# Address offsets modulo 512 bytes for the float32r operands of a Winograd-type matmul, and other dummy products

## The chip, the cores and the metric

The kernel runs on one core of a Trainium2 chip. The metric is the device time of one execution in microseconds; a kernel's time is the median of several executions. A core has five engines that run side by side: TensorE (PE; its weight loads are shown as PEld), VectorE (DVE), ScalarE (ACT), GpSimd (POOL) and SyncE (SP, which here issues transfers). Operands lie in SBUF, 128 partitions wide; an address below is the byte within a partition. TensorE's results go to PSUM.

## The reference

```python
qkv = np.matmul(x, w_qkv)          # x [16, 512, 768], w_qkv [768, 2304], float32
q, k, v = the three column blocks of 768
return np.stack([q, k, v], axis=0)  # [3, 16, 512, 768], float32
```

So it is one product of 8192 x 768 by 768 x 2304, whose columns go to three blocks of the output.

## The kernel before

The 8192 rows of x are worked off in 32 tiles p of 256 rows. The columns of w are cut into two quads q of 1024 columns (two blocks c of 512 each) and a remainder of 256. A product of 256 rows by 768 by 1024 is seen as a 2 x 2 x 2 block product and computed with seven instead of eight half products (Strassen's scheme in Winograd's form). The seven need sums of blocks of x, `s` (five slices k of three parts j, each 128 x 128, float32r), and sums of blocks of w, `t_0` for the first quad and `t_1` for the second (four sums of 3 x 512 columns each, float32r). Two of the seven products use plain bfloat16 blocks (`xb` and `b1`); the other five use float32r: `s` against `t_0`, `t_1` or `b22`. In each, the slice of `s` or `xb` is the stationary operand (the weights that TensorE loads, 128 x 128) and 512 columns of the other are streamed. One half product is three such instructions, over j (lines 211 to 215). The remainder is a plain bfloat16 product (`rem`, line 262).

The first three tiles (`NS = 3`) are computed plainly in bfloat16 by `block` (line 385) while w comes in, since the sums of w aren't ready by then. Before that, dummy products of zeros (`busy`, line 365) keep TensorE going while the first rows arrive: `busy(11)`, then the transposes of the first rows (`turn_rows(0)`, line 167), `busy(4)`, then the casts and the transposes of the next rows (`turn_rows(1)`), then the products of line 385.

From tile 3 on, `two` runs both quads of a tile in an order written out by hand: the first bfloat16 product of each quad, the remainder, the second bfloat16 products, and then ten float32r half products, thirty instructions in a row. `early` issues the next tile's preparation: VectorE transposes x (line 130), POOL makes the bfloat16 copy (line 175) and the five operations of the sums (lines 183 to 187). `last` does the last tile in another order, so that its output can leave early.

The order on each engine is the program's own (the schedule is manual); transfers of w and x and most stores are issued by SP, later loads of x partly by ACT. Tiles are given out by pools in order; the width of 176 of the tile `eye` (line 75) brings all tiles behind it to multiples of 512 bytes:

```python
eye = w_pool.tile([P, 176], bf16, name="eye")[:, :P]
```

In the kernel before, every slice of `s`, `t_0`, `t_1` and `b22` starts at a multiple of 512 bytes: a slice of `s` is 128 float32r, thus 512 bytes, and a slice of the sums of w 2048 bytes.

Of the kernel before, what the change touches and what calls it, by code (L numbers as in the profile page):

```python
# [10 lines left out]
def kernel(  # L11
# [20 lines left out]
    nc = tc.nc  # L32
    P = 128
# [5 lines left out]
    KT = K // P  # L39
    KH = KT // 2  # L40
    KC = K // 4
    NP = M // (2 * P)
    CB = 512
    REM = N3 - 4 * CB
    Q_OFF = (0, 2 * CB + REM)
    R_OFF = 2 * CB
    fp32 = mybir.dt.float32
    f32r = mybir.dt.float32r
# [11 lines left out]
    tq_pool = ctx.enter_context(tc.tile_pool(name="tq", bufs=2))  # L60
    bt_pool = ctx.enter_context(tc.tile_pool(name="bt", bufs=1))
# [7 lines left out]
    s_pool = ctx.enter_context(tc.tile_pool(name="s", bufs=2))  # L69
# [5 lines left out]
    eye = w_pool.tile([P, 176], bf16, name="eye")[:, :P]  # L75
    w_rem = [w_pool.tile([P, KH, REM], bf16, name="w_rem0"), None]

    b1 = [w_pool.tile([P, KT, CB], bf16, name=f"b1_{q}") for q in range(2)]
    b22 = [w_pool.tile([P, KH, CB], f32r, name=f"b22_{q}") for q in range(2)]
    t_0 = w_pool.tile([P, 4, KH, CB], f32r, name="t_0")  # L80
    w_rem[1] = rem_pool.tile([P, KH, REM], bf16, name="w_rem1")
    ts = [[t_0[:, n] for n in range(4)], None]
# [4 lines left out]
    def load_w(dst, j0, nj, off, cols):  # L87
        rows = w_qkv.rearrange("(p j) n -> p j n", j=KT)
        nc.sync.dma_start(dst, rows[:, j0:j0 + nj, off:off + cols])
# [2 lines left out]

    def load_blocks(q, c, nj=KH):
        if q == 0:
            t = tq_pool.tile([P, KT, CB], fp32, name="st0", tag="tq")
            for j in range(0, KT, nj):
                load_w(t[:, j:j + nj], j, nj, Q_OFF[q] + c * CB, CB)
            stage[q, 0, c], stage[q, 1, c] = t[:, :KH, :], t[:, KH:, :]
        else:
            for h in range(2):  # L100
                t = st_pool.tile([P, KH, CB], fp32, name="st1", tag="st")
                load_w(t[:], h * KH, KH, Q_OFF[q] + c * CB, CB)
                stage[q, h, c] = t[:]
# [15 lines left out]
    def load_x(p, other):  # L119
        xin[p] = xin_pool.tile([P, 2 * P // G, KC], fp32, name="xin")  # L120
        t = xin[p]
        rows = x_flat[p * 2 * P:(p + 1) * 2 * P, :].rearrange("(g b) k -> b g k", b=G)
        for n in range(2):
            for h in range(2):
                i = 2 * h + n
                (nc.sync, other)[h].dma_start(t[i * G:(i + 1) * G], rows[:, :, i * KC:(i + 1) * KC])
# [26 lines left out]
    def cast_rows(p, two=True):  # L153
        src = xin.pop(p)
        xc[p] = s_pool.tile([P, 2, K], bf16, name="xc", tag="s")
        for r in range(2):
            halves = (slice(0, K // 2), slice(K // 2, K))
            copy_halves([xc[p][:, r, n] for n in halves], [src[:, r, n] for n in halves], two)

    def turn_rows(p, two=True):  # L160
        c = xc.pop(p)
        xb[p] = xb_pool.tile([P, KT, 2 * P], bf16, name="xb", tag="xb")
        for r in range(2):
            cols = c[:, r, :].rearrange("m (p j) -> m j p", j=KT)
            ps = ps_pool.tile([P, KT, P], bf16, name="ps")
            for j in range(KT):
                nc.tensor.transpose(ps[:, j, :], cols[:, j, :], eye)  # L167
            ks = (slice(0, KH), slice(KH, KT))
            copy_halves(
                [xb[p][:, n, r * P:(r + 1) * P] for n in ks], [ps[:, n, :] for n in ks], two  # L170
            )
# [5 lines left out]
    def sums_x(p):  # L177
        t = xf.pop(p)
        a11, a12 = t[:, :KH, :P], t[:, KH:, :P]
        a21, a22 = t[:, :KH, P:], t[:, KH:, P:]  # L180
        s = s_pool.tile([P, 5, KH, P], f32r, name="s")
        g = nc.gpsimd
        g.tensor_tensor(s[:, 1], a21, a22, op=add)  # L183
        g.tensor_tensor(s[:, 2], s[:, 1], a11, op=sub)  # L184
        g.tensor_tensor(s[:, 3], a11, a21, op=sub)  # L185
        g.tensor_copy(out=s[:, 0], in_=a22)
        g.tensor_tensor(s[:, 4], a12, s[:, 2], op=sub)  # L187
        sr[p] = s
# [5 lines left out]
    def quad(p, q):  # L194
        u = Quad()
        u.p, u.q = p, q
        u.o = o_pool.tile([P, 2, 2 * CB], fp32, name="o", tag="o")
        u.x = u.y = u.z = None
        return u
# [17 lines left out]
    def bank():  # L217
        return ps_pool.tile([P, CB], fp32, name="ps")
# [29 lines left out]
    def rows_of(s, p, lo, hi):  # L248
        return out_flat[s, p * 2 * P:(p + 1) * 2 * P, lo:hi].rearrange("(r m) n -> m r n", m=P)
# [10 lines left out]
    def rem_row(p, r, ps):  # L260
        for j in range(KT):
            nc.tensor.matmul(  # L262
                ps, xb[p][:, j, r * P:(r + 1) * P], w_rem[j // KH][:, j % KH, :],
                start=(j == 0), stop=(j == KT - 1), skip_group_check=True,
            )

    def rem(p):
        ps = ps_pool.tile([P, 2, REM], fp32, name="ps")
        for r in range(2):
            rem_row(p, r, ps[:, r, :])  # L270
        o = or_pool.tile([P, 2, REM], fp32, name="orem")
        nc.scalar.activation(o[:], ps[:], ident)  # L272
        nc.sync.dma_start(rows_of(1, p, R_OFF - H, R_OFF - H + REM), o[:])

# [67 lines left out]


    NS = 3
    zero = xb_pool.tile([P, CB], bf16, name="zero", tag="xb")
    nc.vector.memset(zero[:], 0.0)  # L346
    load_rows(0)
    nc.scalar.activation(tiny[:], zero[:, :1], ident)
    make_identity(nc, eye)
    load_rows(1)  # L350
    load_blocks(0, 0, 1)
    st_rem = o_pool.tile([P, KT, REM], fp32, name="str", tag="o")
    load_w(st_rem[:], 0, KT, R_OFF, REM)
    load_rows(2)
    load_blocks(0, 1)
    load_blocks(1, 0)
    load_blocks(1, 1)
    load_x(3, nc.sync)
    quads = [[quad(p, q) for p in range(NS)] for q in range(2)]

    def busy(n):

        ps = bank()
        for _ in range(n):
            nc.tensor.matmul(ps[:], zero[:, :P], zero[:], start=True, stop=True)  # L365

    def cast(q, h, c, w, eng):

        dst = w[:, h * KH:(h + 1) * KH, :]
        if eng is nc.scalar:  # L370
            eng.activation(dst, stage[q, h, c], ident)
        else:
            eng.tensor_copy(out=dst, in_=stage[q, h, c])
# [40 lines left out]

    nothing = lambda p: None
    busy(11)
    cast_rows(0)
    turn_rows(0)
    busy(4)
    cast_rows(1)  # L420
    cast_k(0)
    cast_k(1)
# [21 lines left out]
    block(1, 0, b1[1], halves(range(6)), cast_next(1, 1, bt1))  # L444
    block(1, 1, bt1, halves(range(6)), nothing)
    rem(2)
    t_1 = [tq_pool.tile([P, 2, KH, CB], f32r, name=f"t_1{n}", tag="tq") for n in range(2)]
    ts[1] = [t_1[n // 2][:, n % 2] for n in range(4)]
    sum_w(1, 1)
    sum_w(1, 2)  # L450
    transpose(3)
    round_x(3)
    sums_x(3)
    sum_w(1, 3)
    sum_w(1, 4)
    dve.tensor_copy(out=b22[1][:], in_=stage[1, 1, 1])

    for p in range(NS, NP):
        def early():
            if p + 1 < NP:  # L460
                transpose(p + 1)
                round_x(p + 1)
                sums_x(p + 1)
            if p + 2 < NP:
                load_x(p + 2, nc.scalar)

        if p < NP - 1:
            two(quad(p, 0), quad(p, 1), early)
        else:
            last(quad(p, 0), quad(p, 1))  # L470
# [30 lines left out]
```

## Time and profile before

| what | value |
|---|---|
| time, median of 3 runs (lowest to highest) | 363.17 us (362.58 to 363.25) |
| profiled execution: span from first to last instruction | 361.3 us |
| mean granted clock of TensorE | 1.000 |
| busy: TensorE / weight loads | 353.4 / 251.0 us |
| busy: VectorE / ScalarE / POOL | 224.4 / 182.9 / 173.9 us |
| float32r products (lines 211 to 215) | 696 + 174 |
| period of one tile in `two` | 10.74 us |

The profile is of one execution, and the page gives its span; its own time isn't listed beside the three runs, whose median is 1.87 us above that span. Busy time of TensorE is not a measure of work, because matmuls are pipelined and a matmul's length overlaps the next one's. The distance between the starts of two matmuls, or of the two weight loads that go with them, is what one costs. In the groups of instructions, a row names the line, the engine, the operation, the tiles written and read, shapes and count, then busy time in us, the mean length in ns, and the idle time in front.

### The profile page before, as it was taken

How to read it: one execution, taken by the hardware profiler on the slowest of the kernel's cores; microseconds unless marked ns; L12 is line 12 of the kernel's file. 1: busy time of each engine (PE TensorE's matmuls, PEld its weight loads, DVE VectorE, ACT ScalarE, POOL GpSimd, SP SyncE). 2: the span in 40 equal slices, each digit the busy share in tenths (PEclk: the TensorE clock that was granted, in tenths of full speed). 3: DMA queues.
4: the chain of work that ended last, by engine and by line, in shares of the span. 5: the costliest groups of instructions: out<-in, count | busy, mean ns of one | idle time of the engine just before them, and what ended most of it. 6: DMA issues, size and time to landing. Idle time of an engine off the chain costs nothing.

```text
span 361.3 us, 5221 instructions
## 1 busy us (share of the span) xinstructions
PE 353.4 (98%) x1765; PEld 251.0 (69%) x1797; DVE 224.4 (62%) x239; ACT 182.9 (51%) x304; POOL 173.9 (48%) x180
## 2 busy tenths in 40 slices
PE   8999999999999999999999999999999999999995
PEld 3644577777777777777777777777777777777763
DVE  3499826765566765566675565676556676556642
ACT  4547555455454545454545445455545454545452
POOL 0001861746664445664445665444665444666410
PEclk9999999999999999999999999999999999999999
DMA  7999869988898999899899999998989899999666
GB/s 298 405 388 373 286 221 359 331 289 295 278 328 301 294 273 294 276 324 315 280 280 290 281 308 309 291 289 278 292 288 321 295 300 271 297 272 339 264 261 232
DMA packets 80617, 108.08 MB, mean 299 GB/s; under 512 B 4816, under 2 KB 60368, under 8 KB 80592
## 3 DMA queue, kind: packets, MB, share of 16 engines
q1 hardware_dynamic: 65184, 96.35, 80.8%
q10 hardware_dynamic: 15408, 11.41, 9.6%
q8 instruction: 14, 0.23, 0.3%
q14 instruction: 11, 0.09, 0.1%
HBM read 32.24 MB, written 75.50 MB: 298 GB/s over the span
## 4 chain that ended last, share of the span: by engine, by line
PE 96%; ACT 1%; issue 1%; ACTq 0%; DVE 0%
PE ps L212 75%; PE ps L262 11%; PE ps L385 9%; PE ps L365 1%; PE ps L167 1%; ACT o L243 0%; ACTq L303 0%; ACT xb L147 0%; ACT orem L317 0%; DVE xb L145 0%; ACT xc L147 0%; ACTq L319 0%; DVE zero L346 0%; ACTq L317 0%
## 5 line engine op out<-in xcount | busy, mean ns | idle before, releaser
L212 PE MATMUL ps<-t,s 128*128 128x512 f32 x696 | 173.8, 398 | 0.0
L212 PEld LDWEIGHTS ps<-t,s 128*128 128x128 f32 x696 | 130.7, 188 | 29.7
L175 POOL CAST xb<-xf 128x1536 bf16<-128x1536 f32 x29 | 43.8, 1510 | 168.3 <-DVE xf L130 156.0
L240 DVE TENSOR_TENSOR o<-o,ps 128x512 f32<-128x512 f32 x58 | 39.9, 688 | 91.2 <-ACT o L239 91.2
L130 DVE STREAM_TRANSPOSE xf<-xin 128x1536 f32<-128x1536 f32 x29 | 85.5, 2950 | 3.7 <-DMA out_dram<-orem 2.1
L212 PE MATMUL ps<-b,xb 128*128 128x512 bf16 x320 | 82.4, 380 | 1.5
L239 ACT ACTIVATE o<-ps 128x512 f32<-128x512 f32 x58 | 34.8, 600 | 44.2 <-PE ps L212 44.2
L212 PEld LDWEIGHTS <-xb 128*128 128x128 bf16 x348 | 31.7, 98 | 35.6 <-issue 7.3
L233 ACT ACTIVATE o<-ps 128x512 f32<-128x512 f32 x58 | 34.9, 601 | 42.1 <-PE ps L212 39.4
L246 DVE TENSOR_TENSOR o<-o,ps 128x512 f32<-128x512 f32 x58 | 39.9, 688 | 21.3 <-PE ps L212 20.2
L212 PE MATMUL ps<-b,s 128*128 128x512 f32 x174 | 48.7, 389 | 0.0
L262 PE MATMUL ps<-w_rem,xb 128*128 128x256 bf16 x384 | 47.2, 273 | 0.0
L243 ACT ACTIVATE o<-ps 128x512 f32<-128x512 f32 x58 | 34.7, 599 | 24.1 <-PE ps L212 21.3
L226 ACT ACTIVATE o<-ps 128x512 f32<-128x512 f32 x58 | 34.7, 598 | 23.8 <-DVE o L246 20.6
L262 PEld LDWEIGHTS <-xb 128*128 128x128 bf16 x384 | 37.4, 98 | 11.2 <-issue 0.5
L230 DVE TENSOR_TENSOR o<-o,ps 128x512 f32<-128x512 f32 x58 | 36.5, 673 | 5.4 <-PE ps L212 4.1
L212 PEld LDWEIGHTS ps<-b,s 128*128 128x128 f32 x174 | 32.7, 188 | 6.8
L184 POOL TENSOR_TENSOR s<-s,xf 128x384 fp32r<-128x384 f32 x29 | 30.0, 1035 | 2.3
L183 POOL TENSOR_TENSOR s<-xf 128x384 fp32r<-128x384 f32 x29 | 30.9, 1064 | 0.0
L185 POOL TENSOR_TENSOR s<-xf 128x384 fp32r<-128x384 f32 x29 | 29.5, 1017 | 0.0
L187 POOL TENSOR_TENSOR s<-xf,s 128x384 fp32r<-128x384 f32 x29 | 29.5, 1016 | 0.0
L272 ACT ACTIVATE orem<-ps 128x512 f32<-128x512 f32 x31 | 18.5, 598 | 20.7 <-PE ps L262 19.5
(36 smaller groups left out, 129.4 us busy)
## 6 DMA issues: line engine op xcount, KB each, us to landing
out_dram<-o SPq DMA_DIRECT2D x62, 768.0 KB, 4.8
out_dram<-o SPq DMA_DIRECT2D x65, 256.0 KB, 4.1
xin<-in_x_dram SPq DMA_DIRECT2D x62, 192.0 KB, 6.9
xin<-in_x_dram ACTq DMA_DIRECT2D x54, 192.0 KB, 4.4
out_dram<-orem SPq DMA_DIRECT2D x31, 256.0 KB, 5.7
st<-in_w_qkv_dram SPq DMA_DIRECT2D x6, 768.0 KB, 13.1
xin<-in_x_dram SPq DMA_DIRECT2D x3, 768.0 KB, 5.7
st<-in_w_qkv_dram SPq DMA_DIRECT2D x6, 256.0 KB, 6.1
```

The lines of the kernel that those rows point to most:

```text
L130: nc.vector.transpose(t[:].rearrange("p j (g b) -> p g j b", b=G), xin.pop(p)[:].rearrange("p g (a j) -> p g j a", a=G),)
L175: nc.gpsimd.tensor_copy(out=xb[p][:], in_=xf[p][:])
L212: nc.tensor.matmul(ps[:], lhs[j], rhs[j], start=(start and j == 0), stop=(j == KH - 1), skip_group_check=True,)
L226: nc.scalar.activation(c11, u.x[:], ident)
L230: nc.vector.tensor_tensor(c11, c11, u.z[:], op=add)
L233: nc.scalar.activation(c12, u.x[:], ident)
L239: nc.scalar.activation(c22, u.x[:], ident)
L240: nc.vector.tensor_tensor(c22, c22, u.y[:], op=add)
L243: nc.scalar.activation(c21, u.x[:], ident)
L246: nc.vector.tensor_tensor(c12, c12, u.y[:], op=add)
L262: nc.tensor.matmul(ps, xb[p][:, j, r * P:(r + 1) * P], w_rem[j // KH][:, j % KH, :], start=(j == 0), stop=(j == KT - 1), skip_group_check= ...
L385: nc.tensor.matmul(ps[n][:], xb[p][:, j, r * P:(r + 1) * P], w[:, j, :], start=(j == 0), stop=(j == KT - 1), skip_group_check=True,)
```

## The change

Four things are changed.

1. A slice of `s` gets 8 more float32r behind it (`P + 8`), which are not used. Each slice then starts 544 bytes after the one before, so 32 bytes further modulo 512.
2. The tiles of the pool `tq` get 16 more elements. The two tiles of `t_1` use it: the first starts 8 elements (32 bytes) into its tile, the second 4 elements (16 bytes). As the second tile of the pool itself now lies 64 bytes off a multiple of 512, `t_1` lies 32 and 80 bytes off; `t_0` and `b22` stay at multiples of 512.
3. `busy(4)`, four bfloat16 dummy products of 512 columns, gives way to `busy_rounded()`: twelve float32r dummy products, three each of 512, 384, 448 and 256 columns. Their operand is a new tile `zeros` in the slot of `bt`, set to zero by POOL ahead of the identity.
4. As a consequence all tiles behind the pool `tq` move: `bt`, `o`, the staging tiles, `xin`, `xf` and `xb` lie 128 bytes off a multiple of 512, and the two tiles of `s` 128 and 96.

```diff
+    PAD = 16
...
-            t = tq_pool.tile([P, KT, CB], fp32, name="st0", tag="tq")
+            t = tq_pool.tile([P, KT * CB + PAD], fp32, name="st0", tag="tq")
+            t = t[:, :KT * CB].rearrange("p (j c) -> p j c", j=KT)
...
-        s = s_pool.tile([P, 5, KH, P], f32r, name="s")
+        s = s_pool.tile([P, 5, KH, P + 8], f32r, name="s")[:, :, :, :P]
...
+    zeros = bt_pool.tile([P, 2 * CB], f32r, name="zeros", tag="bt")
+    nc.gpsimd.memset(zeros[:].bitcast(mybir.dt.uint32), 0)
...
+    def busy_rounded():
+
+        ps = bank()
+        for n in (512, 512, 512, 384, 384, 384, 448, 448, 448, 256, 256, 256):
+            nc.tensor.matmul(ps[:, :n], zeros[:, n:n + P], zeros[:, :n], start=True, stop=True)
...
-    busy(4)
+    busy_rounded()
...
-    t_1 = [tq_pool.tile([P, 2, KH, CB], f32r, name=f"t_1{n}", tag="tq") for n in range(2)]
+    t_1 = [
+        tq_pool.tile([P, 2 * KH * CB + PAD], f32r, name=f"t_1{n}", tag="tq")[
+            :, 8 >> n:(8 >> n) + 2 * KH * CB
+        ].rearrange("p (n j c) -> p n j c", n=2, j=KH)
+        for n in range(2)
+    ]
```

## The prediction

> **What bounds the kernel now.** I read four views in this order: the page's busy times, the chain that ended last, what TensorE waited for, and then two stretches of the timeline, because everything turned out to hang on the spacing of TensorE's products.
>
> ```profile
> span 361.3 us, 5221 instructions
> ...
> PE 353.4 (98%) x1765; PEld 251.0 (69%) x1797; DVE 224.4 (62%) x239; ACT 182.9 (51%) x304; POOL 173.9 (48%) x180
> ...
> PEclk9999999999999999999999999999999999999999
> ...
> PE 96%; ACT 1%; issue 1%; ACTq 0%; DVE 0%
> ...
> L212 PE MATMUL ps<-t,s 128*128 128x512 f32 x696 | 173.8, 398 | 0.0
> L212 PEld LDWEIGHTS ps<-t,s 128*128 128x128 f32 x696 | 130.7, 188 | 29.7
> ...
> L212 PE MATMUL ps<-b,s 128*128 128x512 f32 x174 | 48.7, 389 | 0.0
> ```
>
> TensorE is 96% of the chain, and the other engines and the transfers are behind it. A "mean ns of one" of 398 is no price here, since pipelined products overlap. The price is the distance between starts, and the weight loads give that best, as each starts with the product before it and none of their records is missing. The waits of TensorE and the timeline (start, length, engine, line, operation, count):
>
> ```profile
> PE ps L365 <- DVE zero L346: 1.2, 1, 1.2
> PE ps L167 <- ACT xc L147: 0.5, 1, 0.5
> ```
> ```profile
> 0.73 0.21 POOL masks.py:197 MEMSET eye<- 128x128 bf16 x1 [0.29 <-POOLq L485]
> ...
> 0.86 0.27 DVE L346 MEMSET zero<- 128x256 uint32 x1 [0.86 <-PEq L485]
> ...
> 1.19 4.88 PE L365 MATMUL ps<-zero 128*128 128x512 bf16 x11 [1.19 <-DVE zero L346]
> ...
> 6.95 1.03 PE L365 MATMUL ps<-zero 128*128 128x512 bf16 x4
> ...
> 8.51 0.95 PE L167 MATMUL ps<-eye,xc 128*128 128x128 bf16 x12 [0.53 <-ACT xc L147]
> ...
> 9.30 5.34 PE L385 MATMUL ps<-b,xb 128*128 128x512 bf16 x23
> ```
> ```profile
> 26.05 3.98 PEld L385 LDWEIGHTS <-xb 128*128 128x128 bf16 x19
> ```
> ```profile
> 210.06 4.74 PEld L212 LDWEIGHTS ps<-t,s 128*128 128x128 f32 x21
> ```
> ```profile
> 211.89 2.91 PEld L212 LDWEIGHTS ps<-t,s 128*128 128x128 f32 x13
> ```
>
> Three readings. First, TensorE has only two waits in the whole run, both before 9 us; from 9.30 on it runs product after product, so a delay put in before that stays until the end. Second, a bfloat16 product of 512 columns takes (3.98 - 0.10)/18 = 215.6 ns; a float32r one, in the settled stretch from 211.89, takes (2.91 - 0.19)/12 = 226.7 ns, 11 ns more. Third, that is a settled value. The first loads after a change from bfloat16 stand at 210.06, and eight loads later comes 211.89: 1.83 us, less one bfloat16 product of 0.216 that the first of the eight covers, is 1.614 us for seven products, or 230.6 ns each. So one and the same instruction has more than one price, by some state that settles after eight products. In before every operand of these products, weights and streamed rows, starts at a multiple of 512 bytes.
>
> **The change part by part.** *Dummy products.* Four bfloat16 dummies (6.95 to 7.82 at 0.216 each) leave; twelve float32r ones come, 3 x (512 + 384 + 448 + 256) = 4800 columns. At the settled rate that is 4800/512 x 0.2267 = 2.13 us. The first starts 0.09 later than now, since its weight load takes 188 ns and not 98. They end at 6.95 + 0.09 + 2.13 = 9.17. Before, the transposes of the second rows could start at 8.51, when ScalarE's cast was there; that wait of 0.53 is used up and ends before the dummies do. Twelve transposes at 56 ns (0.67; two of them in this stretch, where neither waits, start 56 apart) bring the first product of line 385 to 9.84, against 9.30: +0.54 us, of which nothing is recovered later, by the first reading. Bounds: at bfloat16's rate the dummies take 2.02 (+0.43); if loads of 188 ns don't overlap each other, the widths 256 and 384 take 188 instead of 113 and 170, +0.28 (+0.82). I take +0.55, in between, since the loads do overlap products of 227.
>
> *POOL's memset of zeros.* 128x1024 before the identity: memsets of 1 and 128 elements took 0.10 and 0.21, so 0.83 ns an element and 0.95 us, estimated. The identity is ready near 2.3 instead of 1.3; it is needed by the transposes at 5.86, so this costs 0. If that cover fails in another way, the VectorE memset of line 346 waits for POOL's to end: then the first eleven dummies start 0.8 later, and the transposes behind them 0.8 later too, but these then run after the clock has risen (427 ns a dummy before, 216 after, at about 6.7 us), which gives back some 0.5. Ends 0 and +0.8; in before the two memsets overlap (0.86 to 0.94), so I take 0. The Trainium skill, SBUF — State Buffer, "Who interferes with whom", says that a VectorE instruction with at most one input, outside its two-port modes, does not contend with GpSimd; that agrees with 0. The tile of zeros takes the slot of bt; the casts into it (line 373) start at 18.70, nine microseconds after the last dummy: 0.
>
> *Padded sums of x.* The five POOL operations write rows of 3x128 at a step of 136 instead of 384 in a row. In before they read such strided rows already (xf) at the same 1.02 to 1.06 us. POOL's work per pair of row tiles is 1.51 + 1.06 + 1.04 + 1.02 + 0.51 + 1.02 = 6.2 us in a period of 10.74, so even 4 us more would be hidden: 0 for the chain. Staging tiles, outputs and xin lie 128 bytes further modulo 512 (one staging tile 64), and VectorE's four sums of the second quad write t_1 at its new offsets; transfers, copies and sums keep lengths and counts, none is moved past another on any queue, and TensorE waits for none of them after 9 us: 0.
>
> *The new offsets in the products.* This is the large unknown: 696 + 174 = 870 products, so each nanosecond is 0.87 us. Each weight slice now lies 32 bytes further modulo 512 than the one before, and t_1 lies 32 and 80 bytes off, so within a quad the distance between the streamed row and the weights that load meanwhile differs from product to product. No row of before has a float32r product at another offset. The nearest rows: 215.6 from below (a bfloat16 product, no extra at all): 870 x -11.1 = -9.7 us. 230.6, the unsettled stretch: 870 x 3.9 = +3.4. The costliest distance of two loads in that stretch is 236 ns: 870 x 9.3 = +8.1 from above. In before the weight slices stand at 0, 512, 1024 and 1536 modulo 2048 while the streamed row stands at 0, and the settled 226.7 is the same for all; nothing shows that an address enters the price at all. I take 0, the row of the same instruction, and keep both ends.
>
> The Trainium skill, SBUF — State Buffer, "Who interferes with whom", says TensorE reads streamed rows and weights through two independent ports and never waits on anyone. By that rule no offset matters and the sum is the dummies' alone. The row speaks partly against it: 226.7 settled and 230.6 unsettled for one instruction means that something does hold these products, and what it is isn't shown.
>
> **Sum.** Span 361.3 + 0.55 = 361.9. The median of the runs shown, 363.17, is 1.87 above that span, so I forecast 363.7 to 363.9: 363.8.
>
> **The rivals.** *Worse: the settled state is lost.* If the price depends on how the two streams lie to each other, an offset that moves with each product keeps it from settling. For it: eight products of other prices after each change of type. Against: nothing ties these to an address. At 230.6: 363.8 + 3.4 = 367.2; at 236, 371.9. It decides (over 0.2%) from an extra of 0.2 ns a product on top of the dummies.
> *Better: the equal offsets are what costs 11 ns.* For it: both streams start together at the same offset, and bfloat16 shows the floor. Against: no distance seen after a change of type was below 225. Half the extra gone gives 363.8 - 4.8 = 359.0, all of it 354.1. It ends below before by 0.2% once a product is 1.5 ns shorter: 1.3 us, less the dummies' 0.55.
> *The sums of x come late.* If the stepped writes made POOL's five operations two thirds slower (4.65 to 8.4 us and more), POOL would fill the period; from there each microsecond is paid 28 times, and one gives 392. Nothing in the rows speaks for it.
> *Two small ones* sit inside the forecast: the memset that delays VectorE (+0.3 to +0.8), and loads that don't overlap (+0.28).
>
> **How the numbers follow.** A change of 0.2% (0.73 us) is about what a measurement can tell. Offsets without effect: 0.40, own range 363.4 to 364.7; of that 0.18 is within 0.2% and 0.22 slower, as either small rival lifts 0.55 over 0.73 and so does a product 0.2 ns dearer. Worse: 0.32, all slower. Better: 0.25, all faster. POOL late: 0.03, slower. So faster 0.25, same 0.18, slower 0.57. Of "better", about 0.10 lies under 358.5 (a product under 220.6); of "worse" and "POOL late", about 0.09 above 368.5 (a product above 232). Between these lies 0.81.
>
> **What the profile after would show.** Right: loads of the sums of x still 226.7 apart in the settled stretch, periods of 10.74, the first product of line 385's successor near 9.85, no wait of TensorE there. Wrong: a period above or below 10.74, which by its thirty float32r products gives the new distance at once; spacings that differ by tile (t_0 against t_1) or by slice would show that the offset is the cause. A first dummy later than 1.19 shows the memset's wait; a wait of TensorE on POOL shows late sums.

## The result and the profile after

The changed kernel takes 367.31 us (four executions, 367.07 to 367.41) against 363.03 before: a ratio of 1.0121, 95% interval 1.0107 to 1.0136, so 4.28 us slower. It lies within the predicted range (358.5 to 368.5) and on the side given the most chance, but not at the forecast of 363.8: it is the rival "the settled state is lost" that came, at its 367.2.

The page of the profile after, with the lines that answer to those of before (line 212 is now line 214):

```profile
span 365.6 us, 5240 instructions
...
PE 358.1 (98%) x1773; PEld 252.3 (69%) x1805; DVE 224.5 (61%) x239; ACT 182.5 (50%) x304; POOL 174.9 (48%) x181
...
PE 97%; issue 1%; ACT 1%; ACTq 0%; DVE 0%
...
L214 PE MATMUL ps<-t,s 128*128 128x512 f32 x696 | 176.7, 402 | 0.0
```

TensorE is still 97% of the chain, every other engine is as busy as before (POOL 1.0 us more, which is the memset of zeros), and the 4.3 us that the span grew lie in TensorE's busy time (+4.7). What TensorE waited for, and the start of the timeline:

```profile
PE ps L369 <- DVE zero L350: 1.2, 1, 1.2
```
```profile
0.73 0.95 POOL L348 MEMSET zeros<- 128x1024 uint32 x1 [0.29 <-POOLq L500]
...
0.86 0.27 DVE L350 MEMSET zero<- 128x256 uint32 x1 [0.86 <-PEq L500]
...
5.86 0.97 PE L169 MATMUL ps<-eye,xc 128*128 128x128 bf16 x12
...
6.64 2.42 PE L375 MATMUL ps<-zeros 128*128 128x512 f32 x12
...
8.91 0.87 PE L169 MATMUL ps<-eye,xc 128*128 128x128 bf16 x12
...
9.62 5.34 PE L395 MATMUL ps<-b,xb 128*128 128x512 bf16 x23
```

The memset of zeros took 0.95 us and did not delay VectorE's, which starts at 0.86 as before. The wait for ScalarE's cast is gone, swallowed by the dummies, as worked out; the first product of the plain blocks comes at 9.62 instead of 9.30. That is 0.32 of the 4.3 us.

The rest is in the float32r products. The chain gives a row tile's period as the distance between the starts of two remainders (line 264, before it 262, twelve products); here one period and the last tile, first after, then before (start and length in us, engine, tile, line, count):

```profile
329.71 1.31 PE ps L264 x12
...
331.29 9.28 PE ps L214 x40
340.57 1.31 PE ps L264 x12
...
342.15 15.54 PE ps L214 x67
```
```profile
325.97 1.31 PE ps L262 x12
...
327.55 9.16 PE ps L212 x40
336.71 1.31 PE ps L262 x12
...
338.29 15.27 PE ps L212 x67
```

The period was 10.74 throughout (325.97 to 336.71); now it alternates between 10.86 (329.71 to 340.57), where the buffer of `s` starts at 96 bytes, and 10.88, where it starts at 128. The remainder takes 1.31 as before; the growth is in the stretches of line 214. The mean, 10.87, is 0.13 above before: 28 x 0.13 = 3.6, the last tile adds 0.27, the start 0.32, together 4.2 of the 4.3 us. The weight loads of one tile:

```profile
201.50 4.81 PEld L214 LDWEIGHTS ps<-t,s 128*128 128x128 f32 x21
```

Twenty distances, the first of which is a bfloat16 product: (4.81 - 0.19 - 0.216)/19 = 231.8 ns, against (4.74 - 0.19 - 0.216)/19 = 228.1 over the same twenty-one loads before, where the last twelve of them stand 226.7 apart. The products no longer settle.

### The profile page after: what moved, and what is told of

The parts are those of the page before. It is cut to its first block, busy times and chain, and to the rows that moved or that the text cites. A ratio compares the mean times of both kernels' runs of the same rounds, so it can differ in the third digit from the quotient of the medians.

```text
span 365.6 us, 5240 instructions
## 1 busy us (share of the span) xinstructions
PE 358.1 (98%) x1773; PEld 252.3 (69%) x1805; DVE 224.5 (61%) x239; ACT 182.5 (50%) x304; POOL 174.9 (48%) x181
## 4 chain that ended last, share of the span: by engine, by line
PE 97%; issue 1%; ACT 1%; ACTq 0%; DVE 0%
PE ps L214 75%; PE ps L264 11%; PE ps L395 8%; PE ps L369 1%; PE ps L375 1%; PE ps L169 1%; ACT o L245 0%; ACTq L305 0%; ACT orem L319 0%; DVE xb L147 0%; ACTq L321 0%; DVE zero L350 0%; ACTq L319 0%
## 5 line engine op out<-in xcount | busy, mean ns | idle before, releaser
L214 PE MATMUL ps<-t,s 128*128 128x512 f32 x696 | 176.7, 402 | 0.0
L214 PE MATMUL ps<-b,s 128*128 128x512 f32 x174 | 49.5, 393 | 0.0
```

The source lines that it names most:

```text
L214: nc.tensor.matmul(ps[:], lhs[j], rhs[j], start=(start and j == 0), stop=(j == KH - 1), skip_group_check=True,)
```

## The experiments

The distance of a product, where it is given in bytes, is the address of its weights less that of the rows streamed against them. Three theories. A: a step of the weights modulo 512 from one product to the next is what unsettles them. B: the distance, modulo some number of bytes, between the weights and the streamed row is. C: offsets don't matter, and the dummies or something else cost the time. All edits are to the kernel before.

**The parts alone.** The dummies with their tile of zeros:

```diff
-    busy(4)
+    busy_rounded()
```

> The kernel before with the twelve float32r dummy products and the memset of zeros alone. By the difference of the two traces at the first product of line 385 (9.62 against 9.30): +0.3 us, so 363.3, and all later periods 10.74. By the prediction's working: +0.55, 363.6.

Measured: 363.21 against 362.62, ratio 1.0014 (1.0005 to 1.0024), +0.59 us. The periods are 10.74 from the second row tile on (the first 10.76). The pad alone:

```diff
-        s = s_pool.tile([P, 5, KH, P], f32r, name="s")
+        s = s_pool.tile([P, 5, KH, P + 8], f32r, name="s")[:, :, :, :P]
```

> The kernel before with the pad of 8 elements behind each slice of the sums of x alone; t_1, t_0 and b22 at multiples of 512. Theory A: nearly the whole loss, +3.0 to +3.9 us (366.0 to 366.9). Theory B: somewhere between 0 and +3.9, as other distances occur than with t_1 shifted. Theory C (the loss is from the shift of t_1 or the dummies): 363.0.

Measured: 366.59 against 362.62, ratio 1.0109 (1.0094 to 1.0124), +3.97 us. The shift of `t_1` alone (with 64 elements of room behind the tiles, so that `s` stays at a multiple of 512):

```diff
+        tq_pool.tile([P, 2 * KH * CB + PAD], f32r, name=f"t_1{n}", tag="tq")[
+            :, 8 + 12 * n:8 + 12 * n + 2 * KH * CB
+        ].rearrange("p (n j c) -> p n j c", n=2, j=KH)
```

> The kernel before with t_1 alone shifted (32 and 80 bytes modulo 256); the sums of x, t_0 and b22 at multiples of 512. By the distance theory twelve of thirty products lie 32 or 80 bytes off (233 and 230 ns in the first sweep) and the others have no eight products in a row to settle in (230.6): +0.10 to +0.17 us a period, +2.9 to +4.7 in all. By the theory that only the weights' own place counts: 0.

Measured: 366.38 against 362.68, ratio 1.0104 (1.0088 to 1.0121), +3.70 us, with periods of 10.86 from the second row tile on:

```profile
209.04 1.31 PE ps L264 x12
...
219.90 1.31 PE ps L264 x12
```

So C falls: either offset alone brings nearly the whole loss. They don't add up, since together with the dummies they cost 4.28 and not 8.3. That `t_1` alone does it, with `s` untouched, shows that it isn't the weights' own place alone that counts.

**A constant offset, another one in each row tile.** If only steps mattered (A), this would cost nothing:

```diff
-        s = s_pool.tile([P, 5, KH, P], f32r, name="s")
+        off = 4 * (p - NS)
+        s = s_pool.tile([P, 5 * KH * P + 128], f32r, name="s")[:, off:off + 5 * KH * P]
+        s = s.rearrange("p (k j c) -> p k j c", k=5, j=KH)
```

> One change to the kernel before: the tile of the sums of x starts 16 bytes further in each row tile p than in the one before it (0 for p = 3, 448 bytes for p = 31); inside a row tile all slices still step by 512 bytes. Theory A (a step between one slice and the next, modulo 512, is what unsettles the products): every period stays at 10.74 us, the span at 361.3. Theory B (what counts is the distance modulo 512 between the weights and the streamed row): the period changes from row tile to row tile, between 10.65 and 10.90, and shows the best offset. Theory C (offsets have nothing to do with it): 10.74 throughout, and the pad alone gives nothing either.

Measured, in one execution: span 364.3. Part of its chain, the starts of the remainders of the row tiles p = 16 to 21; the periods between them are those of p = 16 to 20 (offsets 208, 224, 240, 256 and 272 bytes):

```profile
187.38 1.31 PE ps L264 x12
...
198.25 1.31 PE ps L264 x12
...
209.16 1.31 PE ps L264 x12
...
219.88 1.31 PE ps L264 x12
...
230.62 1.31 PE ps L264 x12
...
241.35 1.31 PE ps L264 x12
```

Periods of 10.87, 10.91, 10.72, 10.74 and 10.73, in one kernel and one execution. A falls: no slice steps modulo 512 inside a tile, and most offsets cost as much as the change. Of the offsets 0 to 416, only 0, 16, 240, 256 and 272 settled at 226.7 ns; the others ran at means of 228.9 to 234.6 ns in their late products (twelve distances of weight loads near the tile's end). And the curve repeats after 256 bytes, not 512: row tiles 16 apart agree within 2 ns (32 and 288: 10.905 both; 80 and 336: 10.880 both), but for the first one (0 and 256: 10.764 and 10.740).

The sweep of pads says the same from the other side:

```diff
+        w = P + (p - NS) % 13
+        s = s_pool.tile([P, 5 * KH * (P + 12)], f32r, name="s")[:, :5 * KH * w]
+        s = s.rearrange("p (k j c) -> p k j c", k=5, j=KH)[:, :, :, :P]
```

> One change to the kernel before: the pad between slices of the sums of x is (p - 3) mod 13 elements, so the slices step by 0, 4, 8 ... 48 bytes modulo 512, each step in two row tiles. Theory A: 10.74 with pad 0 (p = 3, 16, 29), 10.85 to 10.90 with every other pad. Theory B: a period that depends on the pad smoothly, as a mean over the distances that occur, 10.74 to 10.90. Theory C: 10.74 throughout.

Measured, in one execution: span 364.7. Of the three tiles without a pad, only p = 16 ran in 10.75; p = 3 and p = 29 took 10.92 and 10.90, because the two buffers of `s` didn't start at the same offset here, and theirs began 224 bytes off (the first sweep had 10.91 at 224). All padded tiles took 10.81 to 10.94. So a step of zero isn't enough: what counts is the distance that comes with it.

**The other side shifted.** The rows that are streamed lie 64 bytes further, and the weights sweep over all distances. The two gaps move everything behind them by 480 bytes, 32 short of a multiple of 512; that is why `t_1` starts 24 elements (96 bytes) into its tiles, and why an `off` of 24 elements puts the weights at 64:

```diff
+    w_pool.tile([P, 16], fp32, name="gap0")
     b22 = ...
     t_0 = ...
+    w_pool.tile([P, 104], fp32, name="gap1")
...
+        off = 4 * ((p - NS + 8) % 16)
+        s = s_pool.tile([P, 5 * KH * P + 64], f32r, name="s")[:, off:off + 5 * KH * P]
...
+        tq_pool.tile([P, 2 * KH * CB + 64], f32r, name=f"t_1{n}", tag="tq")[:, 24:24 + 2 * KH * CB]
```

> The kernel before with all float32r rows that are streamed (t_0, t_1, b22) 64 bytes further, and the sums of x on a sweep of 16 bytes a row tile over all distances modulo 256. If what counts is the distance between weights and streamed rows, the curve of the periods is that of the first sweep moved by 64 bytes: 10.72 to 10.74 where the weights lie at 48, 64 and 80, 10.91 where they lie at 128, 10.79 at 0. If what counts is where the weights lie by themselves, the curve isn't moved: 10.72 to 10.74 at 240, 0 and 16. If any streamed row off a multiple of 256 is dear by itself: 10.85 and more everywhere.

Measured, in one execution: the curve moved by 64 bytes. Here are the row tiles with the weights at 0 (155.45 to 166.25) and at 64 (198.84 to 209.62):

```profile
155.45 1.31 PE ps L267 x12
...
166.25 1.31 PE ps L267 x12
...
198.84 1.31 PE ps L267 x12
...
209.62 1.31 PE ps L267 x12
```

With the weights at 64 (distance 0) the period is 10.77, settled at 226.7; with the weights at 0 (distance 192) 10.80, where the first sweep had 10.79 at distance 192; at distances 32, 80, 128 and 176 the periods are 10.91, 10.88, 10.89 and 10.83, against 10.90, 10.88, 10.88 and 10.82. So B holds for most distances. Four didn't agree: 16 (10.92 here, 10.73 there), 144 (10.72 here, 10.91 there), 240 (10.77 here, 10.72 there) and 208 (10.90 here, 10.87 there); the others lie within 0.02 us of each other, within 0.03 at distance 0. The fine sweep found the dearer price at 16, 208 and 240 too:

```diff
+        off = (p - 17) % 64
+        s = s_pool.tile([P, 5 * KH * P + 128], f32r, name="s")[:, off:off + 5 * KH * P]
```

> The kernel before; the tile of the sums of x starts at an offset that rises by 4 bytes from row tile to row tile, from -56 (p = 3) over 0 (p = 17) to +56 bytes (p = 31), modulo 256. From the sweep in steps of 16 bytes: settled at 226.7 ns within -16 to +16, periods of 10.72 to 10.74; unsettled at 229 to 234 from 32 bytes on either side. If the distance counts byte by byte, the periods go over gradually and some offset between -16 and +16 may lie below 10.72; if it counts in lines of 16 or 32 bytes, they go in steps.

Measured, in one execution: 10.75 at distance 0; 10.88, 10.84 and 10.81 at 4, 8 and 12; 10.91 at 16; 10.91 to 10.92 at -4, -8 and -12; 10.77 at -16. No lines of 16 or 32 bytes: four bytes are enough, and my expectation of a gradual curve with something better near zero was wrong.

**Two prices at one distance.** Why should 16 cost 10.73 in one run and 10.91 in two others? Three kernels with one distance for all tiles, of which this is the first (60 in place of 4 gives 240; the third has the streamed rows at 64 and the weights at 208):

```diff
+        s = s_pool.tile([P, 5 * KH * P + 64], f32r, name="s")[:, 4:4 + 5 * KH * P]
+        s = s.rearrange("p (k j c) -> p k j c", k=5, j=KH)
```

> The kernel before with the sums of x 16 bytes further in every row tile (16 and 272 modulo 512, as the tiles of s are 256 bytes longer). The coarse sweep settled at 226.7 ns there (10.726 a period), the fine one at 233.3 (10.913). If the state in which a row tile begins decides, all periods take one of the two: 362.3 with the first (28 x -0.014 = -0.4 us), 367.5 with the second. If the distance alone decided, the two sweeps couldn't have differed.

Measured: 367.3 to 367.46 in five executions, and 362.18 in one. The same program has two speeds, 1.4% apart, and the lower one is what 28 periods of 10.726 would give, though there is no profile of it. The profile is of a dear one: all its periods are 10.91, and its late products lie 233.3 ns apart.

> The same with a distance of 240 bytes (-16). Sweeps: 10.723 (settled at 226.7) and 10.774 (a cycle with a mean of 228.3). So 362.2 (28 x -0.017 = -0.5 us) or 363.7 (28 x +0.034 = +1.0).

Measured: 363.02 against 362.61, ratio 1.0007 (0.9994 to 1.002): no difference that is clear. After the first two tiles all periods are 10.74: it settles at 226.7, but only after four products, not at the 10.723 of the sweep.

> All streamed float32r rows at 64 bytes, the sums of x at 208 modulo 256 in every row tile: distance 144. With the streamed rows at 64 the sweep gave 10.721 in both row tiles that had it, with the streamed rows at 0 it gave 10.913. By the first, 362.2 (28 x -0.019 = -0.5 us), a version that would beat both kernels by 0.15%; by the second, 367.5.

Measured: 365.45, ratio 1.0089 (1.0066 to 1.0113); five executions took 365.31 to 365.73, one 368.56. The forecast of 362.2 failed, and so did 367.5; the chain shows both prices in turn:

```profile
198.00 1.31 PE ps L267 x12
...
208.72 1.31 PE ps L267 x12
...
219.64 1.31 PE ps L267 x12
```

10.72, then 10.92 (10.91 without the rounding of the starts), and so on from p = 7 to the end. The buffers of `s`, which lie 256 bytes apart modulo 512 here, don't explain it: p = 10 is dear here and was cheap (10.72) in the kernel with the streamed rows shifted, at the same addresses, and p = 5 is dear in the buffer of the cheap tiles. It looks as if a tile leaves TensorE in a state that decides for the next, though not by cheap and dear alone, since p = 4, 5 and 6 were dear one after the other. That suggested a last test: distance 16 in all tiles but the first, which gets 0.

```diff
+        off = 4 if p > NS else 0
+        s = s_pool.tile([P, 5 * KH * P + 64], f32r, name="s")[:, off:off + 5 * KH * P]
```

> The kernel with distance 16 in every row tile ran at 367.3 in five executions and at 362.18 in one. Here only its first row tile in this scheme (p = 3) lies at distance 0, which settles at 226.7; all others stay at 16. In the coarse sweep each of the two row tiles at 16 came right after one at 0 and settled at 226.7. If the state that one row tile leaves decides for the next, and a settled one keeps it, all executions now stay near 362.2 to 362.6, from a change to one tile of 29. If the distance alone decides, 367.2; if it is chance at each execution, a mixture as before.

Measured: 362.46 in the median of twelve executions, all between 362.12 and 362.95. Its chain, beside that of the kernel with 16 in all tiles:

```profile
57.07 1.31 PE ps L264 x12
...
58.43 9.36 PE ps L214 x41
67.79 1.31 PE ps L264 x12
...
78.52 1.31 PE ps L264 x12
```
```profile
57.01 1.31 PE ps L263 x12
...
58.37 9.55 PE ps L213 x41
67.92 1.31 PE ps L263 x12
...
78.84 1.31 PE ps L263 x12
```

10.73 against 10.91 in row tiles whose addresses, relative to each other, are the same; only the first tile of 29 differs. So the price of a float32r product at this distance is set by the distance and by the rhythm that it comes from. Against before, this kernel is 0.39 us faster (0.9991, interval 0.9982 to 1.0): about what 28 x 0.014 gives, but the interval reaches no change, and it hangs on a state that one tile sets; I wouldn't call it a version that beats the kernel before.

## Why the prediction was right and wrong

- *The dummies*: +0.55 forecast, +0.59 measured alone (interval 0.2 to 0.9). The sum was about right: the later start and the twelve took 2.29 us (first load 6.62, transposes 8.91), against 0.09 + 2.13. The 0.32 between the two profiles is less than what the dummies cost, because their start, 6.95 in the sum, differs from one execution to the next with the moment at which the clock rises: the weight loads of the first transposes go from 110 to about 55 ns apart at 6.7 us in the profile of before, but at 6.2 here. In the kernel with the pad alone, which still has the four bfloat16 dummies, the rise comes already within the first eleven dummies, whose last loads stand 310 and 210 ns apart instead of 430, and the second transposes start at 7.89 instead of 8.51:

```profile
7.89 0.95 PE ps L167 x12
```

  With the four dummies, the first plain product came at 8.89 where the first transposes took 0.83 us (the kernel with the first tile at 0) and at 9.19 where they took 1.11 (streamed rows shifted). For the 0.97 us that they took here that makes about 9.04, an estimate from these two, and 9.62 is 0.58 later.

- *POOL's memset, the slot of bt, padded writes of POOL, moved tiles*: 0 forecast, and the traces show 0. POOL's five operations took 1.07, 1.04, 1.02, 0.51 and 1.03 us as before; the rival of late sums had nothing in it. Its threshold was worked out wrongly besides: POOL would fill the period when the five operations take 10.74 - 1.51 = 9.2 us, twice the 4.65 and not two thirds more.
- *The offsets in the products*: the step that failed. "I take 0, the row of the same instruction" put the settled 226.7 at every offset, because in before the weights stand at 0, 512, 1024 and 1536 without a difference. That row could not tell: all those are the same modulo 256, and the price goes by the distance modulo 256. What stood in its place is the row that I had for the rival, the unsettled 230.6: I priced it at +3.4 and 367.2, and pad or shift alone cost 3.97 and 3.70. In the change itself a period grew by 0.13 us over thirty products, 4.3 ns each, where the sum had 0. The rival's own wording was half right. An offset that moves with each product does keep it from settling; but a constant offset does so as well, at most distances.
- *"The equal offsets are what costs 11 ns"* was wrong the other way round: distance 0 is the one distance at which the products settled at 226.7 in every row tile that had it throughout. No late stretch was below 226.7 at any of the distances tried.
- The range held since its bounds were taken from rows of the trace and not from the favourite, whose 363.8 was 3.5 us too low. That the sign came out as the favourite had it too says little for its mechanism: the dummies, from which it had its "slower", are 0.6 of the 4.28 us. The chance for the rival, 0.32, was too low: one instruction that had shown other prices in seven products after each change of type, in the trace of before, was a reason to doubt that its address could be changed for nothing.

## What to carry to other kernels

Where float32r products follow each other on TensorE (tried here with 128 columns of weights and 512 streamed), keep the weights and the rows streamed at the same offset modulo 256 bytes, and mind it in paddings and in tiles that merely lie behind something of an odd size; four bytes off took 232.5 ns instead of 226.7, 2.6% of a product. Read the price of a product from the distance between weight loads, tile by tile and not as one mean over the run; if it drifts and then settles, ask what it settles to and what could unsettle it. When the rows of a trace all share a property (here, every operand at a multiple of 512), they say nothing of what happens without it, and the nearest other price of the same instruction is a better estimate than zero.

## What the runs showed of the hardware that was not expected

- The price of a 512-column float32r product with 128 columns of weights ranged from 226.7 ns (settled at distance 0) to 236.7 (late mean at distance -44) by four-byte steps in where its operands lie. Bfloat16 products took 216 ns at every offset that came up, 0, 128, 256 and 384 bytes. The Trainium skill, TensorE: Matmul & The Clock Gate, "What happens when you issue a matmul", says that weights and streamed rows come through two independent read ports, so that loading the next weights takes nothing from the running matmul. For bfloat16 the traces agree. For float32r the price changes with the distance between the two, 226.7 to 236.7 ns, which independent ports alone would not give. Whether they meet in SBUF or in TensorE, and whether it is the product's own weights or the next ones that matter, no run here shows.
- The late products fall into rhythms, among them 226.7 each; 233.3 each or on average; 225 and 235 in turn (distance 12, where two take 460). These are 34, 35 and 69 times 6.67 ns, and the periods of the changed kernel, 10.86 and 10.88 us, are 1629 and 1632 times that, as the 10.74 of before is 1611 times. Something with that beat seems to take part; what it is remains open.
- At distances 16, 144, 208 and 240 there is more than one price. At 16 what went before decides: one and the same kernel ran in 362.18 and in 367.3 us, and with its first tile at distance 0 it stayed below 363 in all twelve executions. For 144, 208 and 240 this is likely but not tested. Between the float32r products of two tiles lie twelve bfloat16 products and the remainder, 3.9 us; what carries the state over them, no run here shows.
